# Latent chains in four double steps per stage, with homes of their own, and the light work behind the solve

## The chip, the cores and the metric

One Trainium2 chip, one core of it. The metric is device time in microseconds (us), the median of several executions; less is better. Engines: PE (TensorE, matmuls), DVE (VectorE), ACT (ScalarE), POOL (GpSimd); SP only issues DMAs.

## What is computed

A backbone of two layers over 512 latent tokens and 256 context tokens, 1024 channels, float32. The first layer mixes tokens by an RWKV-7 recurrence of 16 heads, run forwards and backwards, beside a gated short convolution; the second is a convolution module that this change doesn't touch. The recurrence is:

```python
def wkv_scan(S0, r, decay, k, v, kk, a, reverse):
    def step(S, inp):
        r_t, w_t, k_t, v_t, kk_t, a_t = inp
        sa = jnp.einsum("bhvk,bhk->bhv", S, -kk_t)
        S = (S * w_t[:, :, None, :]
             + sa[..., None] * (kk_t * a_t)[:, :, None, :]
             + v_t[..., None] * k_t[:, :, None, :])
        return S, jnp.einsum("bhvk,bhk->bhv", S, r_t)
    S, out = lax.scan(step, S0, (r, decay, k, v, kk, a), reverse=reverse)
    return out, S
...
    yac, S_f, S_b = rwkv_seq(rwkv_prep(hc, rc, kc, vc, *rw), zero, zero, r_k, lnx_w, lnx_b, ctx_out)
...
    ya, _, _ = rwkv_seq(rwkv_prep(h, r, k, v, *rw), S_f, S_b, r_k, lnx_w, lnx_b, True)
    yb = bg * dwconv(cg * xb, sc_w, seg_len)
    y = jnp.concatenate([ya.astype(h.dtype) * jax.nn.silu(za), yb * jax.nn.silu(zb)], axis=-1) @ w_out
```

The context scan gives the states with which the latent scans begin. Both directions (z = 0 and 1) are needed.

## The kernel before

Heads go in pairs, two heads of 64 channels on 128 partitions. There are twelve stages s of a loop: four for the context (two head pairs each), then eight for the latent tokens, one head pair p = s - 4 each. A pair's 512 tokens are cut into 8 chunks of 64. The recurrence is rewritten chunk by chunk: within a chunk a triangular system is solved once, and only a 64 by 64 state H per head and direction is carried from chunk to chunk. A stage is written as a string of letters (STAGE); for a latent stage s, "OSPLMHFC" behind the eight chain steps of pair p:

- S, solve(sts[s+1]): the triangular systems of pair p+1. Xl is transposed from Nt (L737), then 62 operations of DVE in one chain of dependence (L743 a product, L745 a sum, tiles xtmpl, Xl, Yl).
- M, merge of pair p+1: the solved blocks are transposed (L751, L752), 64 and 64 matmuls of 32 by 32 (bank mgl) join them, and copies put the result into the tile E.
- L, light of pair p+2: decay, gates and scaled keys. light0 makes the norms (rnql, rrl, kkl); lightz, once for each direction, the scan Pl (L601), kdl, al, ARl and BKl.
- H, heavy of pair p+2: products pal of ARl and BKl on PE, masked by DVE into E (L686, eight rows in four groups), the transposed keys pbl, and copies of part of E into Nt (L705), which the next solve transposes. E has two tiles, taken in turn, so pairs p and p+2 share one.
- F, finish of pair p: the group norm of the outputs (a small rsqrt of tiny rows on DVE), and po, 32 matmuls that turn them.
- C, conv_branch: four projections of 24 matmuls (pcg, pxb, pbg, pzb) with their weights split into high and low parts (wh by ACT, wl by DVE, L129, L130), and the gated short convolution.
- O: bonus terms. P, prep_lat: POOL's loads of k, v, r and h of pair p+2 from DRAM.

chain_lat(st, i) is one step of a pair's chain: PE forms zol from the state (with E and UV, and with ARl), ACT copies it (Zs, L865), PE multiplies by E into uh, ACT copies that into UV (L872), PE multiplies by BKt into another part of uh, and DVE adds the decayed state HP (L879) into H; ACT then scales H into the next HP (L833). The step's outputs go to onl and are copied (L888) or added. uh stays in the bank uhs[0]; zol, onl, mgl and po take turns on three banks (ps_zo). The solve of pair p+1 needs nothing of pair p's chain.

The instructions of each engine run in the order in which a scheduler puts them. It goes by the order of writing, save where issue_after anchors an operation behind another one: LIGHT_AFTER ties the parts of light, CONV_AFTER the conv branch's projections to steps of the running chain; pinned() keeps a group of matmuls in the order of writing. Each engine waits for the instruction at the head of its queue.

Of the kernel before, what the change touches and what calls it, by code (L numbers as in the profile page):

```python
# [51 lines left out]
def kernel(ctx: ExitStack, tc: tile.TileContext, I: dict, out: bass.AP):  # L52
# [676 lines left out]
    def solve(st):  # L729
# [9 lines left out]
        for i in range(31, 0, -1):  # L739
# [5 lines left out]
            V.tensor_tensor(out=Y[:, :i, c0:], in0=Y[:, :i, c0:], in1=tv, op=ALU.add)  # L745
# [89 lines left out]

    def chain_lat(st, i):
        nm, p = st["nm"], st["p"]
        UV, E, BKt, AR, PC = st["UV"], st["E"], st["BKt"], st["AR"], st["PC"]
# [26 lines left out]
        S.copy(Zs, zo[:, 0:2, :])  # L865
        ahead = values(i + 1) if i < nch - 1 else []
        for h, z in hz:
            cmm(uh[ZR[1 - h], z, :], E[ZR[1 - h], h, z * nch + cs[z], 0:CH], Zs[ZR[1 - h], z, :])
            if ahead:
                ahead.pop(0)()  # L870
        for h in range(2):
            u_ = S.copy(UV[ZR[1 - h], i : 2 * nch - i : 2 * nch - 1 - 2 * i, ZR[h]], uh[ZR[1 - h], 0:2, :])  # L872
# [595 lines left out]
```

## Time and profile before

| | us |
|---|---|
| median of 3 executions | 1387.38 (1385.1 to 1389.39) |
| profiled execution | 1384.0 |
| its span | 1382.2 |
| granted clock of PE, mean | 0.992 |

The profile is a page on the profiled execution, with queries behind it: a timeline of an engine, windows with the busy time of each engine, groups of like instructions, and the chain of waits that ended last. A row of a timeline has start, duration, engine, line, operation, the tile written and those read, shapes and a count; in brackets the idle time ahead of it and what released it. Names in the trace have no buffer numbers: every pair's Xl is Xl. The page's slices are 34.6 us each (1382.2 / 40); latent stages fill slices 14 to 25.

### The profile page before, as it was taken

The numbers are of one execution on the slowest core, as the hardware profiler recorded it, in microseconds if no ns is written. First come the engines' busy times: TensorE is split into PE (matmuls) and PEld (weight loads), VectorE is DVE, ScalarE is ACT, GpSimd is POOL, SyncE is SP. The second block draws the span as 40 slices with busy tenths as digits, with TensorE's granted clock in tenths as the row PEclk, the third lists the DMA queues.
The fourth block names the chain that finished last, engine by engine and source line by source line (L and its number), as shares of the span: only waits on it lengthen the run. The fifth ranks groups of instructions, "written<-read, shape, count | busy, mean of one in ns | idle before, by whom it ended". The sixth has DMA issues, their size and how long they took to land.

```text
span 1382.2 us, 29703 instructions
## 1 busy us (share of the span) xinstructions
PE 1319.8 (95%) x11925; PEld 975.1 (71%) x11925; DVE 986.4 (71%) x2304; ACT 744.4 (54%) x1509; POOL 127.7 (9%) x263
## 2 busy tenths in 40 slices
PE   6999999999998999999999989999999999999998
PEld 2657777777666766666666666677777787788886
DVE  5857879867999499999999998458653653644323
ACT  6546476555765476675756755547742432554222
POOL 4142200001101010101101000010000000000000
PEclk9999999999999999999999999999999999999999
DMA  9865522222323322223222221578621321133232
GB/s 334 272 215 198 161 62 75 92 75 77 96 86 88 97 76 73 78 66 86 77 72 78 76 72 48 187 264 284 203 70 53 122 74 49 62 116 98 92 99 84
DMA packets 139754, 158.54 MB, mean 115 GB/s; under 512 B 15503, under 2 KB 104223, under 8 KB 139497
## 3 DMA queue, kind: packets, MB, share of 16 engines
q1 hardware_dynamic: 123152, 106.47, 24.9%
q0 software_dynamic: 15856, 49.12, 10.9%
q8 instruction: 93, 1.52, 0.5%
q10 hardware_dynamic: 608, 1.06, 0.2%
q14 instruction: 45, 0.37, 0.1%
HBM read 138.33 MB, written 18.28 MB: 113 GB/s over the span
## 4 chain that ended last, share of the span: by engine, by line
PE 46%; DVE 12%; ACT 7%; issue 4%; DMA 4%; POOL 0%; SPq 0%; DVEq 0%; ACTq 0%; POOLq 0%
PE pu L57 12%; PE pz L57 6%; PE f L57 6%; PE pxb L57 3%; PE pcg L57 3%; PE uh L57 3%; PE o L57 2%; DVE E L686 2%; DMA wr<-in_ev_w_out_dram 2%; PE pzb L57 1%; PE zol L57 1%; PE onl L57 1%; PE px L57 1%; PE pc L57 1%; DVE Yl L745 1%
## 5 line engine op out<-in xcount | busy, mean ns | idle before, releaser
L57 PE MATMUL o<-wh,y 128*128 128x512 f32 x248 | 79.8, 396 | 0.0
L743 DVE TENSOR_TENSOR xtmpl<-Xl,Yl 128x126 f32<-128x126 f32 (+22 forms) x248 | 62.3, 251 | 3.1
L745 DVE TENSOR_TENSOR Yl<-Yl,xtmpl 128x126 f32<-128x126 f32 (+22 forms) x248 | 62.2, 251 | 2.9
L1281 ACT CAST ah<-a 64x512 fp32r<-64x512 f32 x32 | 19.8, 618 | 74.8 <-DVE a L1276 74.4
L57 PEld LDWEIGHTS uh<-UV,BKt 128*64 128x64 f32 x704 | 26.4, 136 | 37.6 <-ACT UV L872 27.8
L57 PEld LDWEIGHTS o<-wh,y 128*128 128x128 f32 x248 | 46.2, 188 | 9.5
L57 PE MATMUL pal<-ARl,BKl 64*128 64x128 f32 x512 | 44.5, 295 | 8.7 <-DVE E L686 7.3
L57 PE MATMUL o<-wl,y 128*128 128x512 f32 x124 | 49.7, 401 | 2.3 <-DVE wl L130 2.3
L872 ACT COPY UV<-uh 64x128 f32<-64x128 f32 x128 | 33.3, 260 | 28.9 <-PE uh L57 26.6
L57 PEld LDWEIGHTS pal<-ARl,BKl 64*128 64x128 f32 x512 | 35.3, 191 | 18.8 <-issue 11.1
L130 DVE TENSOR_TENSOR wl<-wr,wh 128x1024 fp32r<-128x1024 f32 x28 | 34.2, 1223 | 19.1 <-ACT wh L129 19.0
L1276 DVE TENSOR_TENSOR a<-pu,a 128x512 f32<-128x512 f32 x16 | 11.0, 691 | 50.0 <-PE pu L57 47.7
L57 PE MATMUL uh<-UV,BKt 128*64 128x64 f32 x704 | 36.5, 232 | 8.7 <-ACT UV L872 4.5
L686 DVE TENSOR_TENSOR E<-pal,maskE 128x512 f32<-128x512 f32 x64 | 42.9, 684 | 0.3
L1233 DVE SCALAR_TENSOR_TENSOR pr<-px,dbe,What 119x512 f32<-119x512 f32 x32 | 22.6, 746 | 26.6 <-PE px L57 26.6
L129 ACT CAST wh<-wr 128x1024 fp32r<-128x1024 f32 x28 | 29.6, 1056 | 19.3 <-DMA wr<-in_ev_w_out_dram 10.1
L57 PEld LDWEIGHTS uh<-Ol,E 64*64 64x64 f32 x512 | 20.3, 133 | 25.8 <-ACT Ol L865 23.6
L879 DVE SCALAR_TENSOR_TENSOR Hl<-uh,PCl,HPl 128x64 f32<-128x64 f32 x112 | 26.2, 276 | 13.7 <-PE uh L57 5.2
L833 ACT ACTIVATE HPl<-Hl,PCl 128x64 f32<-128x64 f32 x96 | 28.1, 340 | 11.0 <-DVE Hl L879 9.8
L745 DVE TENSOR_TENSOR Yc<-Yc,xtmpc 128x126 f32<-128x126 f32 (+22 forms) x124 | 31.5, 254 | 3.1
L743 DVE TENSOR_TENSOR xtmpc<-Xc,Yc 128x126 f32<-128x126 f32 (+22 forms) x124 | 31.5, 254 | 3.0
L57 PEld LDWEIGHTS zol<-Hl,ARl 64*64 64x64 f32 x448 | 18.0, 134 | 21.0 <-DVE xtmpl L743 5.4
(1002 smaller groups left out, 4284.1 us busy)
## 6 DMA issues: line engine op xcount, KB each, us to landing
wr<-in_ev_w_out_dram SPq DMA_DIRECT2D x28, 512.0 KB, 5.2
mwr<-in_mod_w_dram POOLq DMA_DIRECT2D x28, 256.0 KB, 4.2
wrv<-in_ev_w_in_dram SPq DMA_DIRECT2D x16, 256.0 KB, 2.9
ectx<-in_mod_w_dram POOLq DMA_DIRECT2D x16, 256.0 KB, 4.4
wrr<-in_ev_w_in_dram SPq DMA_DIRECT2D x16, 256.0 KB, 2.9
wrza<-in_ev_w_in_dram SPq DMA_DIRECT2D x16, 256.0 KB, 2.8
wrcg<-in_ev_w_in_dram SPq DMA_DIRECT2D x16, 256.0 KB, 2.9
wrxb<-in_ev_w_in_dram SPq DMA_DIRECT2D x16, 256.0 KB, 2.9
```

Source lines behind the costliest of these rows:

```text
L57: env["pe"] = T.matmul(o, lhsT, rhs, start=start, stop=stop)
L129: S.copy(hi, raw)
L130: env["lo"].tensor_tensor(out=lo, in0=raw, in1=hi, op=ALU.subtract)
L686: st["ev"].append(V.tensor_tensor(out=E[:, h, z * NLAT + c0 : z * NLAT + c0 + m, :], in0=pas[h], in1=maskE[:, z * (1 + h) : z * (1 + h) + ...
L743: V.tensor_tensor(out=tv, in0=X[:, :i, i : i + 1].to_broadcast([P, i, m]), in1=Y[:, i : i + 1, c0:].to_broadcast([P, i, m]), op=ALU.mult)
L745: V.tensor_tensor(out=Y[:, :i, c0:], in0=Y[:, :i, c0:], in1=tv, op=ALU.add)
L833: S.activation(t[:, z, :], H[:, z, :], AF.Copy, scale=st["PC"][z][:, i : i + 1])
L872: u_ = S.copy(UV[ZR[1 - h], i : 2 * nch - i : 2 * nch - 1 - 2 * i, ZR[h]], uh[ZR[1 - h], 0:2, :])
L879: h_ = V.scalar_tensor_tensor(out=Hn[:, z, :], in0=uh[:, 2 + z, :], scalar=PC[z][:, i : i + 1], in1=HP[:, z, :], op0=ALU.mult, op1=ALU.add)
L1233: V.scalar_tensor_tensor(out=pr[s][:NPROD], in0=px[s][:NPROD], scalar=dbe[:, 0:1], in1=What[:, n * 512 : n * 512 + 512], op0=ALU.add, op1= ...
L1276: V.tensor_tensor(out=a, in0=pp[1], in1=a, op=ALU.mult)
L1281: S.copy(ahl[s][hr], a[hr])
```

## The change

1. **Order of a stage.** A latent stage becomes "OSMXPLHFC". The new letter X runs four double steps: step i + 4 of pair p and step i of pair p+1, written in turns part by part (chain_lat becomes a generator, together() takes one part of each). Pair 0 does its first four steps alone, pair 7 its last four. All their matmuls go through one pinned().
2. **Homes.** Each parity of pairs has a bank X (one of uhs, for what was zol) and a bank Y (zy0, zy1), in which uh, the product with BKt and the outputs lie side by side. H and HP become fixed tiles. Zs and the outputs go into the pair's used ARt, one tile of double size for both directions; a step's outputs are written and evicted during the next step (outs, closing). merge of latent pairs takes its tiles from the solve's and its bank from uhs.
3. **Anchors.** lightz goes behind the last operation of the solve written last (env["solved"]) instead of behind steps 1 and 4 of the chain. The second projection of the conv branch goes behind step 4 instead of 2.
4. Tiles that shared the AR tag (tokt, dh, early_w, the early weights) are paired in the double-size tiles.

```diff
-LIGHT_AFTER = ((0, None, 0), (None, 1, 4))
+LIGHT_AFTER = ((0, None, 0), (None, "S", "S"))
...
-CONV_AFTER = (0, 2, 7, 6)
+CONV_AFTER = (0, 4, 7, 6)
...
-STAGE = ("KLSMVHvF", "OPLSMHF", "OSPLMHFC")
+STAGE = ("KLSMVHvF", "OPLSMHF", "OSMXPLHFC")
...
-        if st is not None and i is not None:
+        if i == "S":
+            es.enter_context(tc.issue_after(env["solved"]))
+        elif st is not None and i is not None:
...
-        AR = ch3(w("AR", f"AR{nm}{z}"), P)
+        if z == 0:
+            st["ARt"] = w("AR", "AR" + nm)
+        AR = ch3(st["ARt"][:, z * D : z * D + D], P)
...
+            e_ = V.tensor_tensor(out=Y[:, :i, c0:], in0=Y[:, :i, c0:], in1=tv, op=ALU.add)
+        env["solved"] = e_.ins
+        st["Y"], st["XY"] = Y, (Xt, Yt)
...
-        R1, R2, Gs = (w(t, f"{t}m{nm}")[:, 0:512].rearrange("p (a b) -> p a b", b=32) for t in ("kd", "a", "P"))
+        if st["lat"] and st["p"]:
+            Xt, Yt = st["XY"]
+            R1, R2, Gs = (t.rearrange("p (a b) -> p a b", b=32) for t in (Xt[:, 0:512], Xt[:, 512:], Yt))
+        else:
+            R1, R2, Gs = (w(t, f"{t}m{nm}")[:, 0:512].rearrange("p (a b) -> p a b", b=32) for t in ("kd", "a", "P"))
...
-        pg = px = ps_zo("mg" + nm)
+        pg = px = uhs[1 - st["p"] % 2] if st["lat"] else uhs[1]
```

The chain step, with its generator points; the lines that only rename uh, zo and on to the parts of X and Y are left out here:

```diff
         if i == 0:
+            par = p % 2
+            if "y" not in lat2:
+                lat2["y"] = [ps.tile([P, 512], F32, tag="zo", name=f"zy{x}", bufs=2) for x in range(2)]
+                lat2["h"] = [w(t, f"{t}l{x}") for x, t in enumerate(("H", "H", "HP"))]
+            st["py"] = lat2["y"][par]
+            st["xy"] = ch3(uhs[1 - par]), ch3(lat2["y"][par])
+            *st["hn"], st["hp"] = [t[:, par * P : par * P + P].rearrange("p (z x) -> p z x", z=2) for t in lat2["h"]]
             st["HP"] = scale_H(st, st["H"], 0)
...
+        def outs(i, H):
+            cs = (i, nch - 1 - i)
+            oc = (4, 5) if i < nch // 2 else (5, 4)
+            first = [(lambda h=h, z=z: go(Y[ZR[h], oc[z], :], AR[z][ZR[h], cs[z], CH:], H[ZR[h], z, :], z == 1, False))
+                     for z in (1, 0) for h in (1, 0)]
+            then = [(lambda h=h, z=z: go(Y[ZR[h], oc[z], :], E[:, h, z * nch + cs[z], CH:],
+                                         UV[:, z * nch + cs[z], ZR[h]], False, z == 1)) for h, z in hz]
+
...
+            def evict():
+                if i < nch // 2:
+                    S.copy(Q[:, 2 * i + 1 : 32 - 2 * i : 30 - 4 * i, :], Y[:, 4:6, :])
+                else:
+                    o = Q[:, 15 - 2 * i : 18 + 2 * i : 2 + 4 * i, :]
+                    V.tensor_tensor(out=o, in0=Y[:, 4:6, :], in1=o, op=ALU.add)
+
+            return first, then, evict
+
+        def closing(first, then, evict):
+            for f in first + then:
+                f()
+            evict()
...
+        first, then, evict = st.get("outs") or ([], [], lambda: None)
         for z in (1, 0):
             for h in range(2):
-                m0_ = cmm(zo[ZR[1 - h], z, :], AR[z][ZR[h], cs[z], 0:CH], H[ZR[h], z, :], False, z == 0)
-                cmm(on[ZR[1 - h], oc[z], :], AR[z][ZR[1 - h], cs[z], CH:], H[ZR[1 - h], z, :], z == 1, False)
+                m0_ = go(X[ZR[1 - h], z, :], AR[z][ZR[h], cs[z], 0:CH], H[ZR[h], z, :], False, z == 0)
+                if first:
+                    first.pop(0)()
         st.setdefault("anchor", []).append(m0_.ins)
-        Zs = O[:, 8 + 2 * (i % 2) : 10 + 2 * (i % 2), :]
-        S.copy(Zs, zo[:, 0:2, :])
+        yield
+        Zs = Q[:, 2 * i : 31 - 2 * i : 30 - 4 * i, :]
+        S.copy(Zs, X[:, 0:2, :])
+        yield
+        closing([], then, evict)
+        yield
...
+        yield
         for h in range(2):
-            u_ = S.copy(UV[ZR[1 - h], i : 2 * nch - i : 2 * nch - 1 - 2 * i, ZR[h]], uh[ZR[1 - h], 0:2, :])
+            u_ = S.copy(UV[ZR[1 - h], i : 2 * nch - i : 2 * nch - 1 - 2 * i, ZR[h]], Y[ZR[1 - h], 0:2, :])
         h_ = None
+        yield
+        st["outs"] = outs(i, H)
         if i < nch - 1:
...
+            yield
+            Hn = st["hn"][i % 2]
             for z in range(2):
...
+        else:
+            closing(*st["outs"])
         st.setdefault("anc", []).append([x.ins for x in (m0_, u_, h_) if x is not None])
-        for h, z in hz:
-            cmm(on[ZR[h], oc[z], :], E[:, h, z * nch + cs[z], CH:], UV[:, z * nch + cs[z], ZR[h]], False, z == 1)
-        if i < nch // 2:
-            S.copy(O[:, i : nch - i : nch - 1 - 2 * i, :], on[:, 2:4, :])
-        else:
-            o = O[:, nch - 1 - i : i + 1 : 2 * i + 1 - nch, :]
-            V.tensor_tensor(out=o, in0=on[:, 2:4, :], in1=o, op=ALU.add)
+
+    def together(*steps):
+        run = [chain_lat(st, i) for st, i in steps]
+        while run:
+            run = [g for g in run if next(g, run) is not run]
...
-        else:
-            for i in range(NLAT):
-                chain_lat(st, i)
+        elif s == 4:
+            for i in range(NLAT // 2):
+                together((st, i))
         if s == 11:
+            for i in range(NLAT // 2, NLAT):
+                together((st, i))
...
+            elif x == "X":
+                for i in range(NLAT // 2):
+                    together((st, i + NLAT // 2), (sts[s + 1], i))
```

How it moves the work on DVE's queue: before, in the solve of pair 3 (xtmpl3, Xl3, Yl3), rows of pair 2's chain (Hl2) and of pair 4's light (kkl4, Pl40, kdl40, al40) stand between.

```order
L743 TENSOR_TENSOR xtmpl3_7318<-Xl3_7316,Yl3_7317 128x135
L565 SCALAR_TENSOR_TENSOR kkl4_7420<-kl4_7384,cols1_68,rrl4_7418 128x512
L745 TENSOR_TENSOR Yl3_7317<-Yl3_7317,xtmpl3_7318 128x15x9
L601 SCALAR_TENSOR_TENSOR Pl40_7433<-scm_108,sg_109 128x528
L879 SCALAR_TENSOR_TENSOR Hl2_2_7140<-uh0_125,PCl20_5762,HPl2_2_7107 128x64
L879 SCALAR_TENSOR_TENSOR Hl2_2_7140<-uh0_125,PCl21_5791,HPl2_2_7107 128x64
L743 TENSOR_TENSOR xtmpl3_7318<-Xl3_7316,Yl3_7317 128x126
L611 TENSOR_TENSOR kdl40_7440<-kdl40_7440,kl4_7384 128x512
L745 TENSOR_TENSOR Yl3_7317<-Yl3_7317,xtmpl3_7318 128x14x9
L620 SCALAR_TENSOR_TENSOR al40_7431<-al40_7431,kkl4_7420 128x512
```

Now the same solve's end, with merge of pair 3 (Xl3, Yl3, E110) behind it:

```order
L747 TENSOR_TENSOR Yl3_7075<-Yl3_7075,xtmpl3_7076 128x3x15
L745 TENSOR_TENSOR xtmpl3_7076<-Xl3_7074,Yl3_7075 128x30
L747 TENSOR_TENSOR Yl3_7075<-Yl3_7075,xtmpl3_7076 128x2x15
L745 TENSOR_TENSOR xtmpl3_7076<-Xl3_7074,Yl3_7075 128x16
L747 TENSOR_TENSOR Yl3_7075<-Yl3_7075,xtmpl3_7076 128x16
L601 SCALAR_TENSOR_TENSOR Pl40_7513<-scm_108,sg_109 128x528
L758 STREAM_TRANSPOSE Xl3_7074<-Yl3_7075 128x32x16
L611 TENSOR_TENSOR kdl40_7520<-kdl40_7520,kl4_7464 128x512
L759 STREAM_TRANSPOSE Xl3_7074<-Xl3_7074 128x512
L763 COPY E110_4885<-Xl3_7074 32x16x32 x2
L620 SCALAR_TENSOR_TENSOR al40_7511<-al40_7511,kkl4_7500 128x512
L633 SCALAR_TENSOR_TENSOR ARl4_7525<-kkl4_7500,Pl40_7513 128x8x64
```

Pair 2's H has left the solve, and pair 4's light of one direction has gone from the solve's middle into merge.

DVE's queue further on, in the first two double steps of pairs 2 (zy0, PCl20, PCl21, ARl2) and 3 (zy1, PCl30, PCl31), from the last row of light's bonus on:

```order
L616 SCALAR_TENSOR_TENSOR bonl4_7502<-kdl41_7549,cols2_69,bonl4_7502 128x512
L923 SCALAR_TENSOR_TENSOR Hl0_5341<-zy0_5339,PCl20_5916,HPl2_5343 128x64
L923 SCALAR_TENSOR_TENSOR Hl0_5341<-zy0_5339,PCl21_5945,HPl2_5343 128x64
L923 SCALAR_TENSOR_TENSOR Hl0_5341<-zy1_5340,PCl30_6717,HPl2_5343 128x64
L923 SCALAR_TENSOR_TENSOR Hl0_5341<-zy1_5340,PCl31_6746,HPl2_5343 128x64
L617 TENSOR_TENSOR bonl4_7502<-bonl4_7502,rl4_7468 128x512
L633 SCALAR_TENSOR_TENSOR ARl4_7525<-kkl4_7500,Pl41_7542 128x8x64
L881 TENSOR_TENSOR ARl2_5923<-zy0_5339,ARl2_5923 128x2x64
L636 TENSOR_TENSOR ARl4_7525<-rl4_7468,Pl41_7542 128x8x64
L637 SCALAR_TENSOR_TENSOR BKl41_7555<-al41_7540,iPl41_7544 128x8x64
L638 TENSOR_TENSOR BKl41_7555<-kdl41_7549,iPl41_7544 128x8x64
L923 SCALAR_TENSOR_TENSOR Hl1_5342<-zy0_5339,PCl20_5916,HPl2_5343 128x64
```

These four H rows, the output's sum (L881) and five rows of light are what DVE's queue holds between the H rows of the first and of the second double step.

PE's queue in the third of these double steps, with its waits (engine and number of the buffer or semaphore); UV100 and E100 are pair 2's, UV110 and E110 pair 3's:

```order
L57 MATMUL zy0_5339<-UV100_4143,E100_4144 64x64 x4
L57 MATMUL zy1_5340<-UV110_4884,E110_4885 64x64 x4
L57 MATMUL pal4011_7562<-ARl4_7525,BKl40_7526 128x128 [waits PE_49]
L57 MATMUL pal4010_7561<-ARl4_7525,BKl40_7526 128x128
L57 MATMUL zy0_5339<-ARl2_5923,E100_4144 64x64 [waits DVE_49,Activation_49]
L57 MATMUL uh1_126<-UV100_4143,E100_4144 64x64
L57 MATMUL zy0_5339<-ARl2_5923,E100_4144 64x64
```

The outputs of the step before close first (zy0, zy1), a part of pair 4's products (pal40) goes between, and then the product with E into the same bank zy0 waits for DVE and ACT.

More of the change, by code (lines that the diff above doesn't have):

```diff
@@ L249, in start @@
         dft = w("xtmp", "dft")[:31, :NPROD]
-        tokt = [w("AR", f"tok{j}") for j in range(6)]
+        tokt = [t[:, D * j : D * j + D] for t in [w("AR", f"tok{j}") for j in range(3)] for j in range(2)]
         for j in range(6):
@@ L386, in lora @@
             h1 = hp[kt][:, 1:771]
-            dh = w("AR", f"dh{kt}")[:, 0:770]
+            if kt % 2 == 0:
+                dht = w("AR", f"dh{kt}")
+            dh = dht[:, kt % 2 * D : kt % 2 * D + 770]
             V.tensor_tensor(out=dh, in0=hp[kt][:, 0:770], in1=hp[kt][:, 2:772], op=ALU.add)
@@ L786, in values @@
         def values(i):
-            st["zo"] = zo = ps_zo(f"zo{nm}_{i}")
+            st["zo"] = zo = ps.tile([P, 512], F32, tag="zo", name=f"zo{nm}_{i}", bufs=2)
             return [(lambda k=k, z=z, c=c, h=h: cmm(four(zo)[ZR[1 - h], k, :], E[ZR[h], h, z * NLAT + c, :],
@@ L834, in scale_H @@
         return t
+    lat2 = {"go": pinned()}
     def chain_lat(st, i):
-        nm, p = st["nm"], st["p"]
+        p, nch = st["p"], NLAT
         UV, E, BKt, AR, PC = st["UV"], st["E"], st["BKt"], st["AR"], st["PC"]
-        uh, nch = ch3(uhs[0]), NLAT
         if i == 0:
+            par = p % 2
[5 more added lines that the diff above has]
+            *st["hn"], st["hp"] = [t[:, par * P : par * P + P].rearrange("p (z x) -> p z x", z=2) for t in lat2["h"]]
@@ L851, in values @@
             cs = (i, nch - 1 - i)
-            return [(lambda h=h, z=z: cmm(zo[ZR[1 - h], z, :], E[ZR[h], h, z * nch + cs[z], 0:CH],
-                                          UV[ZR[h], z * nch + cs[z], ZR[h]], z == 0, False)) for h, z in hz]
+            return [(lambda h=h, z=z: go(X[ZR[1 - h], z, :], E[ZR[h], h, z * nch + cs[z], 0:CH],
+                                         UV[ZR[h], z * nch + cs[z], ZR[h]], z == 0, False)) for h, z in hz]
+        def outs(i, H):
[12 more added lines that the diff above has]
+            return first, then, evict
@@ L855, in chain_lat @@
+        def closing(first, then, evict):
+            for f in first + then:
+                f()
+            evict()
         if i == 0:
-            for go in values(0):
-                go()
-        zo, on = st["zo"], ch3(ps_zo(f"on{nm}_{i}"))
+            for f in values(0):
+                f()
+        first, then, evict = st.get("outs") or ([], [], lambda: None)
         for z in (1, 0):
             for h in range(2):
-                m0_ = cmm(zo[ZR[1 - h], z, :], AR[z][ZR[h], cs[z], 0:CH], H[ZR[h], z, :], False, z == 0)
-                cmm(on[ZR[1 - h], oc[z], :], AR[z][ZR[1 - h], cs[z], CH:], H[ZR[1 - h], z, :], z == 1, False)
+                m0_ = go(X[ZR[1 - h], z, :], AR[z][ZR[h], cs[z], 0:CH], H[ZR[h], z, :], False, z == 0)
+                if first:
+                    first.pop(0)()
@@ L877, in chain_lat @@
-            Hn = w("H", f"H{nm}_{i}")[:, 0:P].rearrange("p (z x) -> p z x", z=2)
+                go(Y[ZR[h], 2 + z, :], BKt[z][:, cs[z], ZR[h]], UV[:, z * nch + cs[z], ZR[h]])
+            yield
+            Hn = st["hn"][i % 2]
             for z in range(2):
-                h_ = V.scalar_tensor_tensor(out=Hn[:, z, :], in0=uh[:, 2 + z, :],
+                h_ = V.scalar_tensor_tensor(out=Hn[:, z, :], in0=Y[:, 2 + z, :],
                                             scalar=PC[z][:, i : i + 1], in1=HP[:, z, :], op0=ALU.mult, op1=ALU.add)
@@ L910, in finish @@
         rsqrt(rw[:, 8:16], rw[:, 0:8], rw[:, 16:24])
-        V.tensor_tensor(out=O3, in0=O3, in1=rw[:, 8:16].unsqueeze(2).to_broadcast([P, 8, CH]), op=ALU.mult)
-        po = ps_zo(f"po{p}")
+        V.tensor_tensor(out=O3, in0=O3, in1=rw[:, 8:16].rearrange("p (g c) -> p g c", g=2).unsqueeze(3)
+                        .to_broadcast([P, 2, 4, CH]), op=ALU.mult)
         go = pinned()
@@ L1123, in early @@
         else:
-            hl = [w(tag, f"we{k}{x}", F32R) for x in "hl"]
+            t = w(tag, f"we{k}", F32R)
+            hl = [t[:, x * D : x * D + D] for x in range(2)]
         return y, yr, [w("BK", f"wre{k}")[:, 0:D]] + hl
```

36 lines of the change are left out of this document (14 added, 22 removed).

## The prediction

> **What bounds the kernel now.** I read the page's busy times first, then its slices, then the windows from one Xl to the next.
>
> ```profile
> PE 1319.8 (95%) x11925; PEld 975.1 (71%) x11925; DVE 986.4 (71%) x2304; ACT 744.4 (54%) x1509; POOL 127.7 (9%) x263
> DVE  5857879867999499999999998458653653644323
> PE   6999999999998999999999989999999999999998
> L737 DVE STREAM_TRANSPOSE Xl<-Nt x1: 1999/1999/1999, 528.4 to 528.4; 128x1024 f32<-128x1024 f32 x1
> L737 DVE STREAM_TRANSPOSE Xl<-Nt x1: 2043/2043/2043, 820.2 to 820.2; 128x1024 f32<-128x1024 f32 x1
> 587.80:644.80 57.00, 54.45 (x778) 37.93 (x779) 54.16 (x158) 37.66 (x89) 6.74 (x12) 1.00 0.28 77
> 760.10:820.20 60.10, 56.65 (x811) 39.60 (x810) 56.20 (x161) 36.98 (x90) 3.37 (x7) 1.00 0.23 67
> sum 232.40, PE 220.36 PEld 153.50 DVE 219.01 ACT 150.18 POOL 23.58; mean PE 55.09 PEld 38.37 DVE 54.75 ACT 37.55 POOL 5.90
> ```
>
> TensorE looks like the bound of the whole, 95%. In the latent stages (slices 14 to 24) VectorE is as full. Xl, a solve's first operation, comes at 528.4 for pair 2 and at 820.2 for pair 7: five stages of 58.4 us. The windows (four of them, first and last and sum shown; columns: length, then PE, PEld, DVE, ACT, POOL busy, clock, DMA share, GB/s) give 54.75 us of DVE and 55.09 of PE in a mean 58.1. Which one is full in earnest?
>
> ```profile
> 681.66 0.40 PE L57 MATMUL pxb<-hlh,whxb 128*128 128x512 f32 x1
> 681.90 0.39 PE L57 MATMUL pxb<-hll,whxb 128*128 128x512 f32 x1
> 653.74 0.28 DVE L743 TENSOR_TENSOR xtmpl<-Xl,Yl 128x115 f32<-128x115 f32 x1
> 654.05 0.28 DVE L745 TENSOR_TENSOR Yl<-Yl,xtmpl 128x115 f32<-128x115 f32 x1
> ...
> 666.13 0.28 DVE L743 TENSOR_TENSOR xtmpl<-Xl,Yl 128x130 f32<-128x130 f32 x1
> 666.33 0.69 DVE L611 TENSOR_TENSOR kdl<-kdl,kl 128x512 f32<-128x512 f32 x1
> 666.93 0.29 DVE L745 TENSOR_TENSOR Yl<-Yl,xtmpl 128x130 f32<-128x130 f32 x1
> ```
>
> Two stacked projection matmuls start 0.24 us apart and are 0.40 long: the 96 of a stage need 23 us, not 40, so PE has slack that its busy share hides. DVE hasn't: its queue is fed throughout. And it shows what filling is worth there. A solve operation whose successor needs it takes 0.31 us of the queue; with an independent row between, 0.20, and that row 0.60. So DVE's work bounds a stage, 57 of 58 us.
>
> **The change part by part.** First a chain step as it is:
>
> ```profile
> 540.30 0.27 ACT L865 COPY Ol<-zol 128x128 f32<-128x128 f32 x1 [1.42 <-PE onl L57]
> 541.37 0.53 ACT L872 COPY UV<-uh 64x128 f32<-64x128 f32 x2 [0.80 <-PE uh L57]
> 542.63 0.47 DVE L879 SCALAR_TENSOR_TENSOR Hl<-uh,PCl,HPl 128x64 f32<-128x64 f32 x2
> 542.69 0.27 ACT L888 COPY Ol<-onl 128x128 f32<-128x128 f32 x1 [0.79 <-PE onl L57]
> 543.13 0.59 ACT L833 ACTIVATE HPl<-Hl,PCl 128x64 f32<-128x64 f32 x2 [0.18 <-DVE Hl L879]
> 543.97 0.27 ACT L865 COPY Ol<-zol 128x128 f32<-128x128 f32 x1 [0.25 <-PE zol L57]
> ```
>
> From copy to copy 3.67 us, on DVE only the two H rows. Before, eight such steps of pair p (29 us) lie beside solve(p+1): the order rows of before show H between solve operations. The new order ends this. Pair p's steps 4 to 7 are pinned with steps 0 to 3 of pair p+1, and these need E from merge(p+1), which needs the whole solve(p+1). The masks of pair p+2 write the E tile that pair p's step 7 reads last (two tiles, taken in turn), and Xl of p+2 needs those masks. So a stage becomes **one ring: solve, merge, four double steps, masks, Xl**, and I sum it.
>
> (a) *Xl and solve.* No H row is left in it, and light (kd, a, AR, BK: 0.69 us rows) is out as well. The order of pair 3 has 89 rows behind Xl: 62 of the solve, 16 large, 11 small ones of rsqrt. 37 of the 61 solve neighbours are bare (15 before). Xl 2.0; bare ones at their mean 0.25 + 0.03: 10.4; the other 25 at 0.25 - 0.08: 4.2; 16 x 0.60 = 9.6; small ones 11 x 0.1 = 1.1: 27.3. Adding up a stage of before in this way gives 54.6 where the first window has 57.0, so x1.045: **28.6**.
>
> ```profile
> 664.39 1.25 DVE L601 TENSOR_TENSOR_SCAN Pl<-scm,sg 128x528 f32<-128x528 f32 x1
> 687.36 1.11 DVE L751 STREAM_TRANSPOSE kdml<-Yl 128x512 f32<-128x512 f32 x1
> 688.98 0.71 DVE L752 STREAM_TRANSPOSE aml<-kdml 128x512 f32<-128x512 f32 x1
> 689.72 0.85 DVE L756 COPY E<-kdml 32x512 f32<-32x512 f32 x2
> 691.98 0.70 DVE L765 COPY Pml<-mgl 32x512 f32<-32x512 f32 x1
> 695.67 0.69 DVE L770 COPY E<-mgl 32x512 f32<-32x512 f32 x1
> ```
>
> (b) *Solve's end to merge's last copy.* Light, anchored behind the solve's last operation, mixes with merge on DVE. In the new order: two Pl scans 2.36, the transposes 1.03 + 0.63, E copies 0.85, Gs copy 0.62 and 0.5 of wait for its matmuls, six light rows 3.6, last copy 0.61: 10.2, with the factor **10.7**. Merge alone would be 4.5.
>
> (c) *Double steps.* From the last copy to the first H 3.3, two more intervals D, and 4.2 from the third H to the output of p's step 7. DVE has two H pairs and an output row in each, and 6 us of light in all: it idles 8 to 10 us of a stage. D is at least the single step, 3.6. On ACT a double step has two Zs copies, an eviction, four UV copies and four HP scales, by these rows 3 x 0.27 + 2 x 0.53 + 2 x 0.59 = 3.05; Zs of one pair stands behind the HP scales of the other, up to 0.59: +0.5. Outputs now share one home with uh and the H product, so products wait for evictions: +0.2. D = 4.3. Bounds: 3.6 (nothing held) and 7.3 (two steps in series). Sum 3.3 + 8.6 + 4.2 = **16.1**.
>
> The Trainium skill, "PSUM — Partial Sum Buffer", PSUM bank collisions raise a hardware error, asks that engines be guarded against each other by bank and quadrant, which speaks against one home for three products. In the row pair above H (542.63) and the output copy (542.69) run at once, from separate banks, so the trace agrees that separate ones may. By that rule alone D is 4.3, without it 4.1, and the sum 2 us less in all.
>
> ```profile
> 696.37 1.29 DVE L686 TENSOR_TENSOR E<-pal,maskE 128x512 f32<-128x512 f32 x2
> 697.80 1.16 PE L57 MATMUL pal<-ARl,BKl 64*128 64x128 f32 x16
> 700.44 1.28 DVE L686 TENSOR_TENSOR E<-pal,maskE 128x512 f32<-128x512 f32 x2
> 701.16 2.50 ACT L705 COPY Nt<-E 32x512 f32<-32x512 f32 x4 [1.55 <-DVE E L686]
> ```
>
> (d) *Masks to Xl.* Before, merge's rows stood between the groups. Now the first group goes with the last H of p+1, 2.0; three more each wait for the products that refill the freed banks (0.3 + 1.16 + 0.2 + 1.21 = 2.87): 8.6; finish's small rows 0.6; the Nt copies behind the last mask 2.0: **13.2**.
>
> Ring: 28.6 + 10.7 + 16.1 + 13.2 = 68.6, against 58.4: +10.2 in each of five stages, **+51**. PE isn't late in it: behind the double steps it has 95 projections (22 us) and some 11 of small work in 46 us.
>
> *First latent stage.* Four steps of pair 0 run singly beside the start of solve(1), then the ring begins.
>
> ```profile
> 484.54 0.43 DVE L879 SCALAR_TENSOR_TENSOR Hl<-uh,PCl,HPl 128x64 f32<-128x64 f32 x2
> 864.41 1.15 PE po L57 x32
> 908.88 1.15 PE po L57 x32
> ```
>
> From pair 0's first H to Xl of pair 2: 528.4 - 484.5 = 44 us before. After: the solve's remainder 24.4, and (b) to (d), 40: 64.4, **+20**.
>
> *The end.* Before, 88.7 us pass from the last Xl (820.2) to po of pair 7 (908.88; the other po is pair 6's): solve, then eight steps alone. After: solve 28.6 and 0.8 of waits for projection rows, merge and its waits without light 7.2, double steps 15.6, then single steps: step 4's H stands behind finish(6) and two rows of the conv branch in DVE's queue, 9.5; three more 10.9; finish 7.1 up to po: 79.7, a gain of 9 (the waits in it are estimates from the windows above). Seventeen output projections more stand behind po (73 instead of 90 ahead of it), at 0.23: 3.9 back. I take **-5**, between 0 and -9.
>
> *At nothing:* the AR pairing and dh rows (names and offsets, same counts), Q as home of Zs and outputs (same sizes), HP and H in fixed tiles; 2 us either way. Moved with P behind the double steps: POOL's loads of k, v, r and h.
>
> ```profile
> 425.28 3.09 DMA kl<-psp
> ```
>
> A load takes 3.1 us, and the first reader, sq in heavy, comes over 10 us later; without that cover it would cost 3 a stage. Queued behind (c)'s waits on ACT are gates and iPl of light z=1; these are needed by the second mask groups only.
>
> Sum: 1384.0 (profiled execution) + 51 + 20 - 5 = 1450. The median, 1387.4, stands 3.4 above the profiled one: **1454**.
>
> **The rivals.**
> *Lighter loss.* Bare neighbours and evictions cost nothing: 5 us a stage less, about 1425. For it: my factor 1.045 is fitted, not seen. Against: the rows at 653.74. The Trainium skill, "VectorE: DVE Perf Modes", The DRAIN you can't avoid, says the next operation waits for an empty pipe, chained or not; then interleaving gains nothing and (a) is 3.6 smaller: 1433. The trace disagrees: the row at 666.33 starts 0.20 after one of 0.28.
> *Heavier loss.* The two steps of a pair run in series, since PE takes them in written order and each waits for ACT: D = 7.3, 6 to 9 us a stage more, 1490 to 1510.
> *Faster: DVE stays the bound.* If light, conv rows and masks filled the double steps, a stage would need DVE's 54.75 us and no ring: 55.2, five times -3.2, and four single steps at the end instead of eight, -9: about 1360. It decides where DVE has 16 us of queued work during the double steps; the new order shows 6. For it: the wait between merge and heavy would shrink.
> *Nothing.* If PE's 95% is real, or the moves don't take the steps out of the solve's way, 1384 to 1391; the 0.24 us speak against it.
>
> **How the numbers follow.** Forecast 64% (its own range 1430 to 1485), lighter (1393 to 1430) 16%, heavier (over 1485) 7%, faster 9%, within 0.3% (4 us, about what a measurement of this kernel tells from no change) 4%. From 1400 to 1490 leaves out faster, nothing, the lighter end and most of heavier: about 2 in 10. Faster 0.09, same 0.04, slower 0.87.
>
> **What would show it.** Right: Xl of pairs 2 to 7 some 68 us apart, DVE with idle stretches between the last light row and the masks, PE waiting there for ACT and DVE, the solve's DVE window near 28 us without an H row. (c) wrong: H pairs of one pair 3.6 or 7 us apart. (b) wrong: solve's last row to the E copy under 8. Wrong in whole: Xl under 58 us apart, for then the masks don't wait for step 7. What could make it so: E of p+2 starting ahead of p's last read, or a solve far under 28 us once alone on DVE.

## The result, and the profile after

The changed kernel takes 1504.22 us (median of 4, 1492.44 to 1507.7), the kernel before 1387.68 in the same comparison: ratio 1.0836, 95% interval [1.0775, 1.0898]. Slower, as forecast, but by 117 us where 67 were forecast (1454, and nothing over 1490 in the range). Of the changed kernel's eight executions, here and in the last experiment, the two of 1525 us count as slow, and no comparison of kernels rests on them. The profiled execution took 1492.44, its span is 1490.7. Three views of it, first the page's busy times and slices (the second PEclk row is that of the kernel before):

```profile
PE 1350.1 (91%) x11925; PEld 1029.5 (69%) x11925; DVE 1008.8 (68%) x2304; ACT 752.6 (50%) x1509; POOL 127.7 (9%) x263
PE   6999999999989786969696969899999999999998
DVE  5857887777995869695969596755865446444333
PEclk9999999999999888886888689899999999999999
...
PEclk9999999999999999999999999999999999999999
```

The same instructions are run (11925 on PE, 2304 on DVE). The latent stages, slices 13 to 26 of 37.3 us each, have become a wave on both engines, and PE's granted clock falls in them, where the row of before shows 9 throughout. Next the windows from one Xl to the next, pairs 2 to 7, columns as before (the third number from the end is the clock):

```profile
556.87:628.01 71.14, 56.09 (x774) 43.24 (x773) 57.47 (x157) 38.83 (x90) 6.74 (x12) 0.86 0.21 62
628.01:705.46 77.45, 62.88 (x774) 48.60 (x773) 57.54 (x156) 39.17 (x90) 6.74 (x12) 0.76 0.19 56
705.46:778.52 73.06, 58.04 (x774) 44.73 (x773) 57.48 (x156) 38.87 (x90) 6.75 (x12) 0.84 0.20 60
778.52:855.81 77.29, 62.74 (x774) 48.52 (x773) 57.55 (x156) 39.16 (x90) 6.74 (x12) 0.76 0.20 57
855.81:925.85 70.04, 54.76 (x772) 42.35 (x771) 57.17 (x157) 38.00 (x89) 3.25 (x6) 0.88 0.19 53
```

DVE's work is 57.2 to 57.5 us in each, where 54.75 were before; the rest is waiting. Stages of equal work last 70 to 77 us, the longer the lower the clock. Put together by stretch (Xl of pair 1 at 446.46 before and 452.21 after; po of pair 7 at 908.88 and 1014.23):

| stretch | before | forecast | after | after less before |
|---|---|---|---|---|
| up to Xl of pair 1 | 446.5 | 446.5 | 452.2 | +5.7 |
| to Xl of pair 2 | 82.0 | 102.4 | 104.7 | +22.7 |
| five stages to Xl of pair 7 | 291.8 | 343 | 369.0 | +77.2 |
| to po of pair 7 | 88.7 | 79.7 | 88.4 | -0.3 |
| to the end | 473.3 | 477.2 | 476.5 | +3.2 |

Inside a stage the ring is there as described. What is new stands on PE's timeline, at the end of the solve of pair 3 (start, duration, what; in brackets the idle time ahead and its releaser), and in windows cut at the clock's changes:

```profile
580.32 0.39 PE L57 MATMUL pxb<-hlh,wlxb 128*128 128x512 f32 x1
588.63 1.92 PE L57 MATMUL uh<-Xl,E 32*32 32x32 f32 x64 [7.92 <-DVE Xl L759]
591.96 1.92 PE L57 MATMUL uh<-Xl,Yl 32*32 32x32 f32 x64 [1.41 <-DVE Yl L772]
...
584.00:585.00 1.00, 0.00 (x0) 0.00 (x0) 0.90 (x5) 0.00 (x0) 0.00 (x0) 0.63 0.82 240
589.00:604.00 15.00, 11.02 (x263) 9.54 (x262) 11.80 (x23) 9.81 (x25) 1.94 (x4) 0.50 0.15 43
605.00:615.00 10.00, 9.20 (x222) 7.38 (x223) 3.05 (x11) 6.69 (x25) 2.38 (x4) 1.00 0.25 79
660.00:693.00 33.00, 28.40 (x509) 23.34 (x508) 17.15 (x39) 18.83 (x56) 5.06 (x9) 0.50 0.15 44
```

The projections end at 580.7, and PE has nothing for 7.92 us, since merge waits for the solve's end. In the window 584 to 585 the mean clock is 0.63, and in those behind it 0.50: it halves at about 584.3, some 3.6 us after PE's last work (3.8 to 5.1 us in the four stages behind this one). It stays halved from there through merge, whose 64 small matmuls take 1.92 us instead of 1.20, and into the double steps. In this stage it is back at 604.7, in the next only at 693.5, behind the last of them. The H rows on DVE show what that does to a double step, at full clock (605 and 609) and at half (676 and 683). With them stand, in the stage at half clock, the first row behind the solve (656), merge's last copy (666) and the first mask (690):

```profile
605.45 0.48 DVE L923 SCALAR_TENSOR_TENSOR Hl<-zy,PCl,HPl 128x64 f32<-128x64 f32 x2 [0.86 <-ACT UV L913]
609.84 0.48 DVE L923 SCALAR_TENSOR_TENSOR Hl<-zy,PCl,HPl 128x64 f32<-128x64 f32 x2 [1.89 <-ACT UV L913]
...
656.41 1.25 DVE L601 TENSOR_TENSOR_SCAN Pl<-scm,sg 128x528 f32<-128x528 f32 x1
...
666.24 0.69 DVE L777 COPY E<-uh 32x512 f32<-32x512 f32 x1
...
676.90 0.48 DVE L923 SCALAR_TENSOR_TENSOR Hl<-zy,PCl,HPl 128x64 f32<-128x64 f32 x2 [1.11 <-PE zy L57]
...
683.75 0.48 DVE L923 SCALAR_TENSOR_TENSOR Hl<-zy,PCl,HPl 128x64 f32<-128x64 f32 x2 [2.88 <-PE zy L57]
...
690.94 0.69 DVE L688 TENSOR_TENSOR E<-pal,maskE 128x512 f32<-128x512 f32 x1 [3.20 <-PE zy L57]
```

4.39 us against 6.85 (and 5.64 from the first double step of that stage to the second), and the releaser changes from ACT to PE. Merge, though halved too, loses nothing: from the first row behind the solve to the end of merge's last copy 10.5 us pass in each of the five stages (656.41 to 666.93 here), 10.7 by the forecast, for DVE has light's rows to do meanwhile. What differs is the stretch from that copy to the first mask, the double steps: 18.7, 24.0, 20.6, 24.0 and 18.2 us, where 16.1 were forecast. So theory A: the order makes the ring, and the ring leaves PE idle, which halves its clock just where PE is waited for. Its rivals: the clock is a mark of the idle time and costs nothing; the ring itself is longer than summed; the homes or the light cost more than supposed.

### The profile page after: what moved, and what is told of

It is laid out like the page before. It is cut to its first block, busy times and chain, and to the rows that moved or that the text cites. A ratio compares the mean times of both kernels' runs of the same rounds, so it can differ in the third digit from the quotient of the medians.

```text
span 1490.7 us, 29788 instructions
## 1 busy us (share of the span) xinstructions
PE 1350.1 (91%) x11925; PEld 1029.5 (69%) x11925; DVE 1008.8 (68%) x2304; ACT 752.6 (50%) x1509; POOL 127.7 (9%) x263
## 4 chain that ended last, share of the span: by engine, by line
PE 45%; DVE 18%; ACT 6%; issue 4%; DMA 3%; POOL 0%; DVEq 0%; ACTq 0%; SPq 0%; POOLq 0%
PE pu L57 11%; PE pz L57 6%; PE zy L57 6%; PE f L57 5%; PE uh L57 4%; PE o L57 3%; DVE xtmpl L745 3%; DVE Yl L747 3%; PE pal L57 2%; PE pcg L57 1%; PE pbg L57 1%; DVE E L688 1%; DVE Pl L601 1%; ACT UV L913 1%; PE px L57 1%
## 5 line engine op out<-in xcount | busy, mean ns | idle before, releaser
L57 PE MATMUL pal<-ARl,BKl 64*128 64x128 f32 x512 | 54.7, 315 | 5.1 <-DVE E L688 4.9
L57 PE MATMUL uh<-Xl,E 32*32 32x32 f32 x448 | 13.4, 237 | 50.0 <-DVE Xl L759 50.0
L923 DVE SCALAR_TENSOR_TENSOR Hl<-zy,PCl,HPl 128x64 f32<-128x64 f32 x112 | 26.5, 278 | 45.7 <-PE zy L57 28.3
L57 PEld LDWEIGHTS o<-wh,y 128*128 128x128 f32 x248 | 46.6, 189 | 10.5 <-ACT wh L129 0.9
L688 DVE TENSOR_TENSOR E<-pal,maskE 128x512 f32<-128x512 f32 x64 | 42.3, 683 | 16.7 <-PE zy L57 14.7
L57 PEld LDWEIGHTS pal<-ARl,BKl 64*128 64x128 f32 x512 | 40.9, 205 | 17.4 <-issue 9.8
L57 PEld LDWEIGHTS uh<-Xl,E 32*32 32x32 f32 x448 | 12.5, 151 | 53.0 <-DVE Xl L759 53.0
L913 ACT COPY UV<-zy 64x128 f32<-64x128 f32 x128 | 33.3, 260 | 22.2 <-PE zy L57 20.5
L57 PE MATMUL uh<-UV,E 64*64 64x64 f32 x512 | 32.6, 280 | 12.8 <-DVE E L777 12.8
L129 ACT CAST wh<-wr 128x1024 fp32r<-128x1024 f32 x28 | 29.6, 1057 | 21.1 <-PE o L57 10.0
L707 ACT COPY Nt<-E 32x512 f32<-32x512 f32 x32 | 19.8, 618 | 40.3 <-DVE E L688 40.0
L57 PE MATMUL zy<-UV,BKt 128*64 128x64 f32 x448 | 30.5, 278 | 5.9 <-ACT UV L913 5.8
L57 PEld LDWEIGHTS uh<-UV,E 64*64 64x64 f32 x512 | 25.6, 180 | 14.0 <-DVE E L777 13.7
```

The lines of the kernel that those rows point to most:

```text
L57: env["pe"] = T.matmul(o, lhsT, rhs, start=start, stop=stop)
L129: S.copy(hi, raw)
L688: st["ev"].append(V.tensor_tensor(out=E[:, h, z * NLAT + c0 : z * NLAT + c0 + m, :], in0=pas[h], in1=maskE[:, z * (1 + h) : z * (1 + h) + ...
L707: S.copy(Nt[rs], E[rs, h, :, 32 * b : 32 * b + 32])
L923: h_ = V.scalar_tensor_tensor(out=Hn[:, z, :], in0=Y[:, 2 + z, :], scalar=PC[z][:, i : i + 1], in1=HP[:, z, :], op0=ALU.mult, op1=ALU.add)
```

## The experiments

**Fill on PE, first try.** Matmuls that nobody reads are added behind the solve's last four steps:

```diff
+            if st["lat"] and st["p"] and i < 5:
+                for _ in range(6):
+                    d_ = mm(uhs[1 - st["p"] % 2], hlat[0][:, 0, 0:P], hlat[0][:, 0, :], True, True)
+                    tc.add_manual_dep(d_.ins, e_.ins.name, ...)
```

> 24 matmuls of 512 columns that nobody reads (six behind each of the solve's last four steps) are added on PE in every latent solve from pair 1 on; they fill the 7.9 us in which PE stood idle ahead of merge (580.7 to 588.6 in the changed kernel's profile). Theory A (PE's granted clock halves 3.7 us after PE falls idle and stays halved through merge and most of the double steps): clock back near 1.00 in the latent stages, the intervals between the Xl of pairs 2 to 7 from a mean of 73.8 us to 68 to 70, merge's 64 matmuls 1.2 us again instead of 1.92, time 1460 to 1472, though PE does more. Rival B (the halved clock costs nothing, the double steps wait for ACT and DVE): 1500 to 1510, intervals 71 to 77 as before.

1519.03 us (median of 4), slower than the changed kernel and above both ranges. The mean interval is 74.2, the clock 0.943; the first latent stage alone is 11.8 us longer than in the changed kernel (116.5 for 104.7). PE's rows and windows behind the fill, in the solve of pair 3, tell why:

```profile
598.27 1.20 PE L57 MATMUL uh<-Xl,E 32*32 32x32 f32 x64 [0.41 <-DVE Xl L765]
601.79 1.20 PE L57 MATMUL uh<-Xl,Yl 32*32 32x32 f32 x64 [2.32 <-DVE Yl L778]
605.19 0.69 PE L57 MATMUL uh<-UV,E 64*64 64x64 f32 x8 [2.20 <-DVE E L783]
...
599.00:603.00 4.00, 1.67 (x94) 1.45 (x88) 3.92 (x8) 2.57 (x6) 0.00 (x0) 1.00 0.01 4
603.00:613.00 10.00, 7.13 (x128) 5.92 (x128) 7.72 (x16) 6.71 (x20) 2.26 (x5) 0.52 0.19 59
```

Merge itself runs at full clock now (1.20), but in its gaps PE is busy 1.67 us of 4, and at 603 the clock halves all the same. In this stage the fill moved the fall from ahead of merge to the first double step. From merge's last copy to the first mask the five stages take 21.1 us in the mean, as in the changed kernel: merge at full clock gained nothing, and the double steps were at half clock as before. So the run decided between neither theory; it showed that merge's gaps are enough for the fall.

**Fill with needed work.** `CONV_AFTER = (0, 4, 7, 6)` becomes `(0, 4, 4, 6)`, so that the projection pbg may run in the solve.

> Only CONV_AFTER goes from (0, 4, 7, 6) to (0, 4, 4, 6): the projection pbg may run before merge, so PE has 5.6 us of needed work where it stood idle. Theory A: the rest of the idle time, 2.3 us, is below the 3.7 us after which the clock fell; clock near 1.00, Xl intervals 67 to 70 us, time 1450 to 1470. Rival B (clock costs nothing): 1495 to 1510. Rival C (the projections are missing as filler elsewhere, and the clock falls in the masks or the double steps instead): clock below 0.95, time 1475 to 1500.

1484.27 us (ratio 1.0729 [1.0677, 1.0781] to the kernel before, where the changed kernel's was 1.0836), 20 below the changed kernel; mean interval 72.4; clock 0.949. These are rival C's figures, but not its place of the fall: the earlier projections all end earlier, and PE again has nothing ahead of merge, where the clock falls as before. So this run, too, left theories A and B undecided.

```profile
578.00:586.00 8.00, 0.00 (x0) 0.00 (x0) 7.49 (x23) 1.43 (x4) 0.00 (x0) 0.71 0.22 65
586.00:598.00 12.00, 7.76 (x179) 6.51 (x183) 10.04 (x16) 8.23 (x16) 1.08 (x2) 0.50 0.12 45
```

**The homes alone**, in the old order: STAGE "OSPLMHFC", LIGHT_AFTER (None, 1, 4), CONV_AFTER (0, 2, 7, 6), and

```diff
-        elif s == 4:
-            for i in range(NLAT // 2):
+        else:
+            for i in range(NLAT):
                 together((st, i))
         if s == 11:
-            for i in range(NLAT // 2, NLAT):
-                together((st, i))
```

> The changed kernel with the stage order, the light anchors, the conv anchors and the single steps of before; kept are the homes: one bank for uh, the product with BKt and the outputs, X and Y by parity, Q in AR, double-size AR, outputs closed a step later, merge in the solve's tiles. Theory A (the whole loss lies in the order, and the homes cost nothing in the latent stages): Xl intervals 57 to 60, time 1385 to 1395, of it up to 5 us in the context stages, where the changed kernel was late by 5.3 us at the first Xl. Rival D (sharing a bank makes each step longer and the chain, now 8 x 4.2 us, outlasts the solve): intervals 61 to 65, time 1405 to 1430.

1397.66 us against 1384.15, ratio 1.0099 [1.0067, 1.013]; mean interval 59.3, to Xl of pair 2 89.0 instead of 82.0. The intervals are those of theory A, the time lies 2.7 us above its range: the homes are not free, though near it, and the first latent stage alone is 7 us longer. First and last H of a chain beside a solve, of before and with the homes:

```profile
657.98 0.43 DVE L879 SCALAR_TENSOR_TENSOR Hl<-uh,PCl,HPl 128x64 f32<-128x64 f32 x2
681.23 0.47 DVE L879 SCALAR_TENSOR_TENSOR Hl<-uh,PCl,HPl 128x64 f32<-128x64 f32 x2
...
662.20 0.48 DVE L923 SCALAR_TENSOR_TENSOR Hl<-zy,PCl,HPl 128x64 f32<-128x64 f32 x2
688.82 0.48 DVE L923 SCALAR_TENSOR_TENSOR Hl<-zy,PCl,HPl 128x64 f32<-128x64 f32 x2 [0.24 <-PE zy L57]
```

Seven H, six intervals: 3.88 us each before, 4.44 with the homes. The step is longer by 0.56; beside the solve most of it is hidden. Whether the shared bank or the written order on PE makes it longer was not separated.

**The light alone**, in the kernel before: LIGHT_AFTER `(None, 1, 4)` becomes `(None, "S", "S")`.

> The kernel before with one thing of the change: light z=0 and z=1 anchored behind the solve's last operation. Eight single steps still run beside the solve. Theory A (light behind the solve takes the filling out of the solve, 3.6 us of DVE a stage, and leaves all of its 9 us to stand between solve and masks, while PE idles): intervals 62 to 67, time 1405 to 1440. Rival E (only the double steps cost, light may stand anywhere): intervals 58 to 60, time 1385 to 1395.

1399.86 us, ratio 1.01 [1.0069, 1.0131]; mean interval 59.3, to Xl of pair 2 93.2 (+11). Beside running chains, light behind the solve costs 1 us a stage, not 4 to 8: theory A's price for this part was wrong, and rival E, which has the order of the double steps as the main loss, is nearer: its intervals were met, its time was missed by 5 us.

**Fill on PE, second try.** Six matmuls behind each of the solve's last four steps, as before, and eight, with this line, behind each half of merge (m_ is its last matmul; busy adds unread matmuls into the bank of the pair's later outputs):

```diff
+        busy(8, st, m_, False)
```

> Fill on PE that nobody reads, 40 matmuls of 512 columns a latent pair: six behind each of the solve's last four steps, eight behind the first and eight behind the second 64 of merge, all into the bank of the pair's own later outputs. With the first fill alone the clock still halved, only later: 5 us behind the fill's end, in merge's gaps. Theory A (each us at half clock costs about 0.27 us, from 1492 us at a mean clock of 0.933 and 1508 us at 0.915 of the changed kernel's own runs): clock of the latent stages 0.95 to 1.00, Xl intervals 67 to 69.5, merge's matmuls 1.2 us, time 1450 to 1475 with up to 15 us lost to the fill in the first latent stage. Rival B (what the clock takes is hidden behind DVE and ACT; the ring is 72 to 74 us long at any clock): 1490 to 1520.

1475.57 us, 28.7 less than the changed kernel, although PE does 280 matmuls more (12205). Against the kernel before, run beside each, the loss falls from 116.5 us to 90.8. The windows, and one stage on DVE (start of solve, first row behind it, merge's last copy, three H, first mask, next Xl):

```profile
632.79:702.21 69.42, 62.36 (x816) 46.64 (x815) 57.51 (x156) 38.65 (x90) 6.71 (x12) 1.00 0.21 63
702.21:772.35 70.14, 62.98 (x812) 47.59 (x811) 57.51 (x156) 38.81 (x90) 6.72 (x12) 0.98 0.22 63
...
632.79 2.06 DVE L747 STREAM_TRANSPOSE Xl<-Nt 128x1024 f32<-128x1024 f32 x1 [0.98 <-ACT Nt L707]
661.29 1.25 DVE L601 TENSOR_TENSOR_SCAN Pl<-scm,sg 128x528 f32<-128x528 f32 x1
671.01 0.69 DVE L789 COPY E<-uh 32x512 f32<-32x512 f32 x1 [0.23 <-ACT E L789]
674.96 0.97 DVE L935 SCALAR_TENSOR_TENSOR Hl<-zy,PCl,HPl 128x64 f32<-128x64 f32 x4
679.13 0.47 DVE L935 SCALAR_TENSOR_TENSOR Hl<-zy,PCl,HPl 128x64 f32<-128x64 f32 x2 [0.60 <-PE zy L57]
684.04 0.47 DVE L935 SCALAR_TENSOR_TENSOR Hl<-zy,PCl,HPl 128x64 f32<-128x64 f32 x2 [1.89 <-ACT UV L925]
688.63 0.69 DVE L688 TENSOR_TENSOR E<-pal,maskE 128x512 f32<-128x512 f32 x1 [2.08 <-PE zy L57]
702.21 2.05 DVE L747 STREAM_TRANSPOSE Xl<-Nt 128x1024 f32<-128x1024 f32 x1 [1.20 <-ACT Nt L707]
```

The clock is 0.98 to 1.00, and the five intervals are 69.4 to 70.2, mean 69.75: theory A, just beyond the upper edge of what it gave (69.5 us, 1475); rival B falls. Solve 28.5, light and merge 10.4 (to the copy's end), double steps to the mask 16.9, masks 13.6: the ring, as summed, at full clock. The rest of the 73.8 us, 4.1 a stage, is what the clock took, at the least: in three of the five stages, those in which the clock still falls for a few microseconds, light and merge take 11.8 instead of 10.4. By parts, in the mean of the five, the double steps fall from 21.1 us to 16.7 and the masks from 13.8 to 13.5; the solve is the same (28.4).

**Fewer double steps.** In the stage loop four becomes 2, or 1; the steps between run singly, written ahead of the next solve:

```diff
...
-                for i in range(NLAT // 2):
-                    together((st, i + NLAT // 2), (sts[s + 1], i))
+                for i in range(2):
+                    together((st, i + NLAT - 2), (sts[s + 1], i))
```

> The changed kernel with two double steps per stage instead of four: the last two steps of pair p with the first two of pair p+1; the four steps between run singly beside the next solve. Ring theory (each double step adds its 4.4 to 5.2 us to the ring, and a single step beside the solve only its two H rows, 0.4 us of DVE): Xl intervals shorter by 7 to 11 than the changed kernel's 73.8, so 63 to 67; time 1415 to 1450. Rival F (the ring is set by light and merge behind the solve, not by the double steps): intervals 70 to 74, time 1480 to 1505.

> The same with one double step. Ring theory: a further 3.5 to 5.5 us off each interval, 59 to 62; time 1395 to 1420. Rival F: intervals over 68.

1441.85 us with two (interval 65.8, clock in the stages 0.85 to 0.90), 1410.63 with one (61.9, clock 0.95 to 1.00): the ring theory's figures both times, and not rival F's. Each double step taken out of the ring shortens it, and raises the clock; which of them did how much, the next run separates.

> The kernel with two double steps, with the fill of 8 + 8 unread matmuls behind merge's two halves (none in the solve's end, where PE has the single steps and projections). With four double steps at full clock an interval was 69.75 us. Theory A (ring at full clock): two double steps fewer, 2 x 4.5, and four single steps' H rows on DVE in the solve, 1.6, give 62 to 63.5; clock 0.95 to 1.00; time 12 to 20 us below that of two double steps without fill (1441.85). Rival B (its 65.8 us are the ring, and the half clock costs nothing there): intervals 65 to 67, time 1437 to 1450.

1418.81 us, 23 below the same kernel without fill (30.8 above the kernel before, run beside it, for 57.1). Its windows, first and last of five alike:

```profile
548.03:609.22 61.19, 57.31 (x787) 40.62 (x786) 56.87 (x157) 38.11 (x90) 6.26 (x12) 1.00 0.25 72
794.41:855.77 61.36, 57.80 (x790) 40.93 (x789) 56.84 (x157) 37.38 (x89) 3.42 (x7) 1.00 0.21 62
```

At full clock four double steps give 69.75 and two 61.55: 4.1 us of ring for each, net of the single steps that take their place. The clock's part is 4.3 us a stage here (65.8 to 61.55), all of it between merge's last copy and the first mask (13.2 to 8.9). Theory A holds; interval and gain both go somewhat beyond what it gave (62 to 63.5, and 12 to 20 us). No version of these is faster than the kernel before.

**Light back into the solve**, in the changed kernel: LIGHT_AFTER `(None, "S", "S")` becomes `(None, None, None)`.

> The changed kernel with lightz not anchored: it goes into the solve again (16 large rows between solve operations), merge stands alone. By the rows: the solve gains 9 us, merge loses 6, and the five rows that lay in the double steps (nothing on the path) are paid now: +3 us a stage at equal clock; PE's gap ahead of merge grows from 8 to some 17 us, so the clock is down at least as long. Xl intervals 75 to 79, time 1510 to 1540. Rival G (light behind the solve is the loss, the double steps are not): intervals 62 to 68, time 1420 to 1460.

1563.54 us, ratio 1.1308. The intervals are 84.9 to 85.4, at a clock of 0.72 (one window, and PE's first row of merge in it):

```profile
654.57:739.93 85.36, 65.72 (x774) 50.30 (x773) 56.13 (x158) 39.33 (x90) 6.70 (x12) 0.72 0.17 51
...
693.93 1.92 PE L57 MATMUL uh<-Xl,E 32*32 32x32 f32 x64 [10.52 <-DVE Xl L759]
```

Worse than expected, by 6 us a stage. With the double steps in place, light behind the solve is no loss but a gain. Rival G falls. PE's wait ahead of merge is 10.5 us (7.9 in the changed kernel, and not the 17 that I had supposed). The 11.5 us a stage more than the changed kernel's 73.8 divide so: the solve 37.5 for 28.4 (+9.1, as expected), light and merge 8.4 for 10.5 (-2.1, where -6 was expected; merge alone, at half clock, is not covered by light's rows), the double steps 24.0 for 21.1 and the masks 15.3 for 13.8. All five stages have the 24.0 us that the changed kernel has in its two longest half clocks, so some 7 us are DVE's rows and 4.4 lie where the half clock costs.

**The changed kernel again.**

> The changed kernel once more, unaltered, to see what of its time repeats. If the halved clock follows PE's idle time, clock and Xl intervals repeat (0.91 to 0.94, mean interval 72 to 76), time 1490 to 1510; the start up to the first Xl (399.4 us in its first profile, 394.1 before) differs by several us, up or down, if it hangs on chance dips of the clock and not on the change: 392 to 404.

Its profiled execution took 1500.06 us, mean clock 0.924, intervals 70.7 to 78.4 (mean 75.1), all as expected. The four took 1497.02 to 1525.68 (median 1512.65), where 1490 to 1510 were expected. Of this kernel's executions up to 1508 the longer are those of lower clock (1492.44 at 0.933, 1497.02 at 0.926, 1500.81 at 0.925, 1507.64 at 0.915). The first Xl stands at 397.1. In the eleven profiled executions of the other experiments and of the first comparison, whose kernels differ ahead of that point in little or nothing, it stands anywhere from 392.1 to 403.0 (at 394.1 and 394.2 in the two that have the old homes).

## Why the prediction was right in kind and wrong in size

- **What bounds a stage: right.** The ring is there with its four parts, DVE idles in it, and PE's stacked projections leave PE idle. Of the marks named beforehand these hold: no H in the solve, its window 28.3 us (556.87 to 585.19), DVE idle between the last light row and the masks. The first doesn't: Xl was to come every 68 us or so, and comes every 70.0 to 77.5.
- **The ring's sum: right at full clock.** Forecast 28.6 + 10.7 + 16.1 + 13.2 = 68.6; with the fill 28.5 + 10.4 + 16.9 + 13.6 = 69.4, and 69.75 in the mean of five. So the serial order costs 11.4 us a stage at full clock (69.75 less 58.35), for 10.2; the rivals "lighter" (1425) and "faster" (1360) fall with it, the form of "lighter" in which interleaving gains nothing by the solve's 28.3 to 28.5 us, where it would have 25.0. The first latent stage was +22.7 for +20.
- **The step that failed: term (c), the double steps, by way of "PE isn't late in it".** That sentence counted PE's work (33 us in 46) and took its rate as given, 1.00 in the windows of before. But in those windows PE was busy 54 to 57 of 57 to 60 us. The idle time that the new order leaves ahead of merge halves the clock, and the double steps, where DVE and ACT wait for PE, run in part or in whole at half clock: D is up to 6.85 for 4.3, and (c) 18.2 to 24.0 us (mean 21.1) for 16.1, against 16.7 with the clock kept up. The term for the clock was missing from the sum. It is at least 20 us in the first profiled execution (5 x 4.1), about 27 in the second (5 x 5.3); the fill takes 25.7 off the loss in the median.
- **The median.** I put it 3.4 us above the profiled execution, as before. It lies 11.8 above, and the longer executions have the lower clock: the time that passes until it returns differs from stage to stage and run to run.
- **The heavier rival** (7%) reached the measured time for another reason. It had the two steps run in series, D = 7.3. At full clock D is 4.2 to 4.9, so they do run side by side; 6.85 was measured at half clock only.
- **The end: wrong by 9.** Up to po of pair 7 a gain of 9 was forecast, and it is 0.3. The wait behind finish(6) was right (9.1 us for 9.5), but two terms were short: the two chains take 18.5 us from merge's copy to the last H, for 15.6, at half clock for the first 7; and the single steps behind them took 5 to 6 us each, for 3.6. Their H rows on DVE stand between the weights' rows of the output projection:

```profile
990.13 0.47 DVE L923 SCALAR_TENSOR_TENSOR Hl<-zy,PCl,HPl 128x64 f32<-128x64 f32 x2 [0.56 <-PE zy L57]
993.18 1.22 DVE L130 TENSOR_TENSOR wl<-wr,wh 128x1024 fp32r<-128x1024 f32 x1 [1.35 <-ACT wh L129]
995.06 0.47 DVE L923 SCALAR_TENSOR_TENSOR Hl<-zy,PCl,HPl 128x64 f32<-128x64 f32 x2 [0.32 <-PE zy L57]
1000.86 0.48 DVE L923 SCALAR_TENSOR_TENSOR Hl<-zy,PCl,HPl 128x64 f32<-128x64 f32 x2 [0.23 <-issue]
```

- **At nothing: the homes** cost 13.5 us in the old order (1397.66 against 1384.15), where 2 either way were allowed; a step is longer by 0.56 us, not by the 0.2 that D had for it. In the ring that is inside D. The start's +5.7 is within what comes and goes between runs; whether a part of it is the change's stays open.

The 50 us between forecast and median add up: clock in the ring 20, the median's distance from the profile 8, ring 6, end 8, start 6, first stage 2.

## What to carry to other kernels

A change that puts parallel chains in series is priced by the ring of dependences that it closes, stage by stage; here that sum held to two per cent at full clock. But TensorE's rate was not fixed: 8 us of idle time ahead of a latency chain halved its clock for 17 to 38 us. So when an order leaves such a gap, the chain is to be priced at half clock as well. Unread work in the gap and in merge gave back a fifth of the loss here; needed work was tried in one place, and left a gap at least as long. A part that is a loss by itself (light behind the solve, 1%) may be a gain once another part is there (59 us lost without it), so parts are undone one at a time from both ends.
